# The last token block's final norm shared between VectorE, ScalarE and GpSimd, and the first products reordered, in a one-core encoder layer

## The chip, the cores and the metric

The kernel runs on one core of a Trainium2 chip. The time is the device time of one execution in microseconds; a version's time is the median of its runs. The engines are named as in the profile: PE (TensorE), ACT (ScalarE), DVE (VectorE), POOL (GpSimd), and SP (SyncE), whose queue issues most of the DMAs.

## What is computed

One encoder layer on 512 tokens of width 1024 in float32. Two token mixers (a windowed attention with sinks, and a mixture of dilated windows) are merged by sigmoid gates; a residual and a norm follow; then a SwiGLU feed-forward and the second residual and norm, whose output is the result:

```python
proj = h @ w_in[l]
qa, ka, va, qb, kb, vb = jnp.split(proj, SPLITS, axis=-1)
...
y = mixed @ w_out[l]
h = layer_norm(DN_ALPHA * h + y, ln1_g[l], ln1_b[l])
f = (jax.nn.silu(h @ w_ff_gate[l]) * (h @ w_ff_up[l])) @ w_ff_down[l]
h = layer_norm(DN_ALPHA * h + f, ln2_g[l], ln2_b[l])
```

with `layer_norm(x) = (x - mu) * rsqrt(var + eps) * g + b` over the 1024 columns.

## The kernel before

Every float32 operand is split into a high part (a rounded copy, on ACT or DVE) and a low part (the difference, on DVE), and a product is three matmuls: high by high, and each high by the other's low. A 128x512 tile is one `slot` (`sl` in the profile); weights come in units of 128x1024 from `wpack`, in halves of 512 columns.

The order of instructions on each engine is not written by hand. Every operation is handed to `Program.op` with the engines that may take it, a modelled cost, the tokens it reads and writes, and a priority; `Program.run` then plays the program through with these costs (a list scheduler), and each engine takes the ready operation with the lowest priority number. It also models the DMA path: `dma` holds two clocks, that of the issuing queue and that of the transfers, both 0 at the start. What the model thinks is ready first stands first in an engine's order, and on the chip each engine then keeps that order, whatever arrives first.

**The head.** The first three products, called k, q and r (the first unit of the keys, `U_KA`, and the first two of the queries, `U_QA` and `U_QA + 1`), run over the eight 128x512 tiles of x transposed (`xT`; `x` in the profile once they are split). Their weights' first halves come in pieces of 256 columns (`half_unit_by`, `CUTS`), with fixed priorities from the table `FIRST`; k's first piece is issued from ACT's queue, the rest from SP's. `FIRST["q", 0]` and `FIRST["r", 0]` begin with -999.7 and -999.6. The matmuls are those of L941. Before them PE runs eight matmuls on zeros (L409). After them come unit q2 (`feat_k`, L454 to L456), then the value weights (`token_values`, L610 to L629). The two rotary tables (`ropec`, `ropes`), the masks (`maska`, `maskb`) and the sinks (`nsink`) are loaded in the same stretch.

**The tail.** The last stage, `tok_major` with `fine` set, sums the down projection for four blocks `t` of 128 tokens, each with two column halves `j`, and norms each block when its sums are complete: residual (L1105), statistics (L1108, L1111), the root on ACT (L1113), `(z - mu) * g` on DVE (L1119, "centre" below), the reciprocal of the root on DVE (L1122), then `z * r + b` on DVE (L1134, "finish" below). In blocks 1 and 2 (`BY_POOL`) that finish is instead a scaling on ACT (L1127) and an addition of the bias on POOL (L1129). Each piece is stored by a DMA of SP's queue (`store`, L1493). For the last block the second half is cut in two pieces of 256 columns, so there are three pieces: 512, 256, 256.

At the program's end (L1595) each engine drains and all meet twice, with POOL as the one that collects and releases.

Of the kernel before, what the change touches and what calls it, by code (L numbers as in the profile page):

```python
# [12 lines left out]
AF = mybir.ActivationFunctionType  # L13
ALU = mybir.AluOpType

P = 128
S = 512
# [4 lines left out]
NR = 4  # L22
# [29 lines left out]
BRANCHES = "a0 a1 a2 b0 a3 b1 b2 a4 b3 b4 a5 b5 b6 a6 b7 a7"  # L52
N_BEGIN = 2
N_HALF = 3
N_LAST1, N_LAST, BY_POOL = 5, 4, (1, 2)
BANKS = dict(dense=3, s=2, tb=2, o=1, d=8)
UNITS = 2
D_BANK = "s"
SPIN = 4

CUTS = ((0, 256), (256, 512))
FIRST = {("k", 0): (-1000, -998.4), ("q", 0): (-999.7, -998.2), ("r", 0): (-999.6, -998.1),
         ("k", 1): (-997.7,), ("q", 1): (-997.5,), ("r", 1): (-997.4,),
# [34 lines left out]
class Program:  # L98
# [16 lines left out]
    def op(self, alts, fn, reads=(), writes=(), prio=0.0, after=(), abs_prio=None, moves=0.0):  # L115
        o = Op()
        o.urgent = self.urgent
        o.alts, o.fn = alts, fn
        o.prio = (self.T + prio if abs_prio is None else abs_prio, len(self.ops))
        o.ready, o.done, o.eng = 0.0, None, None  # L120
        deps = set(a for a in after if a is not None)
        for t in reads:
            deps.update(self.writer.get(t, ()))
        for t in writes:
            deps.update(self.writer.get(t, ()))
            deps.update(self.readers.get(t, ()))
        deps.discard(o)
        for t in reads:
            self.readers.setdefault(t, []).append(o)
        for t in writes:  # L130
            self.writer[t] = [o]
            self.readers[t] = []
        o.bufs, o.new = [], []
        o.strict, o.moves = self.strict, moves
        for t in list(reads) + list(writes):
            b = self.buf_of(t)
            if b not in o.bufs:
                o.bufs.append(b)
                b.users += 1
        o.succ = []  # L140
        o.left = len(deps)
        for d in deps:
            d.succ.append(o)
        self.ops.append(o)
        return o
# [25 lines left out]
    def run(self):  # L171
# [2 lines left out]
        pending = {e: [] for e in engines}  # L174
        times = [0.0]
        frees = []
        dma = [0.0, 0.0]

        def add(o):
            heapq.heappush(times, o.ready)  # L180
# [19 lines left out]
        while n_left:  # L200
# [5 lines left out]
            while frees and frees[0][0] <= now:  # L206
                _, _, b = heapq.heappop(frees)
# [68 lines left out]
def act(n, psum=False, extra=0):  # L276
    return (0.052 if psum else 0.094) + 0.000833 * n + 0.093 * extra


def dve(n, fast=False, extra=0.0):  # L280
    return 0.069 + (0.00074 if fast else 0.00104) * n + extra
# [7 lines left out]
def hybrid_layer(ctx: ExitStack, tc: tile.TileContext, wpack, xT, xtok, sink, bgate,  # L289
# [77 lines left out]
    def half_unit_by(u, j, cuts, prios):  # L367

        st, h, l = slot(F32, "ws"), slot(F32R, "whl"), slot(F32R, "whl")
        pieces[h] = pieces[l] = cuts  # L370
        for (c0, c1), ap in zip(cuts, prios):
            w = c1 - c0
            if ap == -1000:
                op([(ACT, 0.4)], lambda e, c0=c0, c1=c1: nc.scalar.dma_start(
                    st.t[:, c0:c1], wpack[u, :, j * S + c0:j * S + c1]), writes=[(st, c0)], abs_prio=ap,
                   moves=0.73 * w / S)
            else:
                op([(SP, 0.73 * w / S)], lambda e, c0=c0, c1=c1: nc.sync.dma_start(
                    st.t[:, c0:c1], wpack[u, :, j * S + c0:j * S + c1]), writes=[(st, c0)], abs_prio=ap)
            op(cp_alts(w), lambda e, c0=c0, c1=c1: copy(e, h.t[:, c0:c1], st.t[:, c0:c1]),  # L380
               reads=[(st, c0)], writes=[(h, c0), (l, "room", c0)], abs_prio=ap)
            op([(DVE, dve(w))], lambda e, c0=c0, c1=c1: nc.vector.tensor_tensor(
                l.t[:, c0:c1], st.t[:, c0:c1], f32(h.t[:, c0:c1]), op=ALU.subtract),
               reads=[(st, c0), (h, c0)], writes=[(l, c0)], abs_prio=ap)
        return h, l
# [672 lines left out]
    def ln_vectors(gsrc, bsrc, after):  # L1058
# [5 lines left out]
                res.append(b)  # L1064
        return res[0:2], res[2:4]

    def tok_major(nk, last, us_of, u0, g, b, finish, fine, alpha=ALPHA):

        acc = {(t, j): bank("d") for t in range(NR) for j in range(2)}

        def kmm(k, t, j, c0, c1, us, wu, ps):
            wh, wl = wu[j]

            def go(e):
                a0, a1 = us[0].t[:, t * P:(t + 1) * P], us[1].t[:, t * P:(t + 1) * P]
                o = ps.t[:, c0:c1]
                mm(o, a0, wh.t[:, c0:c1], start=(k == 0), stop=False, skip_group_check=True)  # L1077
                mm(o, a0, wl.t[:, c0:c1], start=False, stop=False, skip_group_check=True)  # L1078
                mm(o, a1, wh.t[:, c0:c1], start=False, stop=(k == nk - 1), skip_group_check=True)  # L1079

            op([(PE, 3 * pe(c1 - c0))], go, reads=[*us, wh, wl], writes=[ps])
            pr.T += 3 * pe(c1 - c0)

        for k in range(nk - last):
            us = us_of(k)
            wu = unit(u0 + k)
            for t in range(NR):
                for j in range(2):
                    kmm(k, t, j, 0, S, us, wu, acc[t, j])
        res = [(k, us_of(k), unit(u0 + k, LOOK if last < nk else LOOK_E)) for k in range(nk - last, nk)]  # L1090
        for t in range(NR):
            pr.urgent = t == NR - 1
            st = stats()
            pieces = [(0, 0, S), (1, 0, S)]
            if fine and t == NR - 1:
                pieces[1:] = [(1, 0, S // 2), (1, S // 2, S)]
            toks = []
            for n, (j, c0, c1) in enumerate(pieces):
                ps, z = bank("d") if c0 else acc[t, j], xt[t, j]
                for k, us, wu in res:  # L1100
                    kmm(k, t, j, c0, c1, us, wu, ps)
                tok = (z, c0)
                toks.append(tok)
                w = c1 - c0
                op([(DVE, dve(w))], lambda e, z=z, ps=ps, c0=c0, c1=c1: nc.vector.scalar_tensor_tensor(  # L1105
                    z.t[:, c0:c1], z.t[:, c0:c1], alpha, ps.t[:, c0:c1], op0=ALU.mult, op1=ALU.add),
                   reads=[z, ps], writes=[tok], prio=NOW)
                op([(DVE, dve(w))], lambda e, z=z, st=st, n=n, c0=c0, c1=c1: nc.vector.bn_stats(  # L1108
                    st.t[:, 6 * n:6 * n + 6], z.t[:, c0:c1]), reads=[tok], writes=[(st, n)], prio=NOW)
            np_ = len(pieces)  # L1110
            op([(DVE, 0.14)], lambda e, st=st, np_=np_: nc.vector.bn_aggr(st.t[:, 32:34], st.t[:, 0:6 * np_]),  # L1111
               reads=[(st, n) for n in range(np_)], writes=[(st, "a")], prio=NOW)
            op([(ACT, 0.2)], lambda e, st=st: nc.scalar.activation(  # L1113
                st.t[:, 34:35], st.t[:, 33:34], AF.Sqrt, bias=eps.t[:, 0:1]), reads=[(st, "a"), eps],
               writes=[(st, "s")], prio=NOW)
            for (j, c0, c1), tok in zip(pieces, toks):
                z = xt[t, j]
                op([(DVE, dve(c1 - c0, extra=0.06))], lambda e, z=z, st=st, j=j, c0=c0, c1=c1:
                   nc.vector.scalar_tensor_tensor(  # L1119
                       z.t[:, c0:c1], z.t[:, c0:c1], st.t[:, 32:33], g[j].t[:, c0:c1], op0=ALU.subtract,  # L1120
                       op1=ALU.mult), reads=[tok, (st, "a"), g[j]], writes=[tok], prio=NOW)
            op([(DVE, 0.1)], lambda e, st=st: nc.vector.reciprocal(st.t[:, 35:36], st.t[:, 34:35]),  # L1122
               reads=[(st, "s")], writes=[(st, "r")], prio=NOW)
            for (j, c0, c1), tok in zip(pieces, toks):
                z = xt[t, j]
                if fine and t in BY_POOL:
                    op([(ACT, act(S, extra=1))], lambda e, z=z, st=st: nc.scalar.activation(  # L1127
                        z.t, z.t, AF.Copy, scale=st.t[:, 35:36]), reads=[tok, (st, "r")], writes=[tok], prio=NOW)
                    op([(POOL, 1.25)], lambda e, z=z, j=j: nc.gpsimd.tensor_tensor(z.t, z.t, b[j].t, op=ALU.add),  # L1129
                       reads=[tok, b[j]], writes=[tok], prio=NOW)  # L1130
                    finish(t, j, c0, c1, tok)
                    continue
                op([(DVE, dve(c1 - c0, extra=0.06))], lambda e, z=z, st=st, j=j, c0=c0, c1=c1:
                   nc.vector.scalar_tensor_tensor(  # L1134
                       z.t[:, c0:c1], z.t[:, c0:c1], st.t[:, 35:36], b[j].t[:, c0:c1], op0=ALU.mult,
                       op1=ALU.add), reads=[tok, (st, "r"), b[j]], writes=[tok], prio=NOW)
                finish(t, j, c0, c1, tok)
        pr.urgent = False
# [461 lines left out]
```

## Time and profile before

| | us |
|---|---|
| median of 3 runs (lowest to highest) | 779.84 (779.28 to 780.75) |
| the profiled execution | 779.7 |
| its span, first to last instruction | 777.9 |
| busy in the span: PE, DVE, ACT, POOL | 766.2, 652.7, 479.7, 122.2 |

A row of the timeline gives start and length in us, the engine (with q: its sequencer, which only issues or waits), the line, the operation, tile written <- tiles read, the shapes, how many it merges, and in brackets the idle time ahead of it and what ended that. A row of busy times by stretch gives the stretch and its length, each engine's busy time and instructions, PE's granted clock, the DMA engines' mean share and GB/s. A row of groups gives line, engine, operation, tiles, shapes and count, then busy us and mean ns of one, then idle us before. A row of one line's sequencer instructions gives the count, min/median/max ns, and the first and last start.

### The profile page before, as it was taken

The numbers are of one execution on the slowest core, as the hardware profiler recorded it, in microseconds if no ns is written. First come the engines' busy times: TensorE is split into PE (matmuls) and PEld (weight loads), VectorE is DVE, ScalarE is ACT, GpSimd is POOL, SyncE is SP. The second block draws the span as 40 slices with busy tenths as digits, with TensorE's granted clock in tenths as the row PEclk, the third lists the DMA queues.
The fourth block names the chain that finished last, engine by engine and source line by source line (L and its number), as shares of the span: only waits on it lengthen the run. The fifth ranks groups of instructions, "written<-read, shape, count | busy, mean of one in ns | idle before, by whom it ended". The sixth has DMA issues, their size and how long they took to land.

```text
span 777.9 us, 13378 instructions
## 1 busy us (share of the span) xinstructions
PE 766.2 (99%) x4470; PEld 675.9 (87%) x4470; DVE 652.7 (84%) x1373; ACT 479.7 (62%) x1057; POOL 122.2 (16%) x288
## 2 busy tenths in 40 slices
PE   8999999999999999999999999999999999999995
PEld 6888888888888888888888899999999999999984
DVE  6378999888989898696686999797988889888697
ACT  6257785778787688693341767556655566555631
POOL 0011010101005204200020010232102331122002
PEclk9999999999999999999999999999999999999998
DMA  8745232203223224354472497699867987789102
GB/s 274 211 138 196 79 105 82 90 28 110 83 87 102 81 86 153 109 183 141 136 208 63 116 245 221 142 200 203 222 188 161 228 184 212 179 214 216 43 1 108
DMA packets 68848, 113.35 MB, mean 146 GB/s; under 512 B 8620, under 2 KB 17068, under 8 KB 68780
## 3 DMA queue, kind: packets, MB, share of 16 engines
q1 hardware_dynamic: 57116, 91.40, 36.4%
q0 software_dynamic: 11520, 20.98, 16.5%
q8 instruction: 35, 0.57, 0.3%
q14 instruction: 33, 0.27, 0.1%
q10 hardware_dynamic: 144, 0.13, 0.1%
HBM read 104.87 MB, written 4.72 MB: 141 GB/s over the span
## 4 chain that ended last, share of the span: by engine, by line
PE 96%; DVE 1%; ACT 1%; DMA 1%; issue 0%; SPq 0%; DVEq 0%; ACTq 0%
PE ps L454 10%; PE ps L455 10%; PE ps L456 10%; PE ps L1314 9%; PE ps L1313 9%; PE ps L1312 9%; PE ps L1441 4%; PE ps L1442 4%; PE ps L1443 4%; PE ps L675 3%; PE ps L1077 3%; PE ps L1079 3%; PE ps L1078 3%; PE ps L941 2%; PE ps L627 2%; PE ps L629 2%
## 5 line engine op out<-in xcount | busy, mean ns | idle before, releaser
L333 ACT ACTIVATE sl<-sl 128x512 fp32r<-128x512 f32 (+4 forms) x456 | 247.9, 571 | 79.7 <-DMA sl<-wpack 20.4
L1196 DVE TENSOR_TENSOR sl<-sl,sl 128x512 fp32r<-128x512 f32 (+3 forms) x304 | 169.8, 602 | 11.2 <-ACT sl L333 7.2
L333 ACT ACTIVATE sl<-ps 128x256 f32<-128x256 f32 (+4 forms) x188 | 81.6, 450 | 106.3 <-PE ps L1314 65.6
L454 PE MATMUL ps<-x,sl 128*128 128x512 f32 x280 | 110.9, 396 | 0.0
L455 PE MATMUL ps<-x,sl 128*128 128x512 f32 x280 | 109.5, 391 | 0.0
L456 PE MATMUL ps<-x,sl 128*128 128x512 f32 x280 | 109.3, 390 | 0.0
L354 DVE TENSOR_TENSOR sl<-sl,sl 128x512 fp32r<-128x512 f32 x114 | 75.5, 685 | 8.8 <-ACT sl L333 7.8
L1266 POOL DMA_DIRECT2D sl<-wpack x44 | 40.7, 1008 | 267.1 <-DMA sl<-wpack 144.1
L1312 PE MATMUL ps<-x,sl 128*128 128x256 f32 x264 | 74.8, 283 | 0.0
L1314 PE MATMUL ps<-x,sl 128*128 128x256 f32 x264 | 74.7, 283 | 0.0
L1313 PE MATMUL ps<-x,sl 128*128 128x256 f32 x264 | 74.7, 283 | 0.0
L1196 DVE TENSOR_TENSOR sl<-sl,ps 128x512 f32<-128x512 f32 (+1 forms) x78 | 47.3, 610 | 25.4 <-PE ps L1314 16.2
L456 PEld LDWEIGHTS ps<-x,sl 128*128 128x128 f32 x280 | 52.6, 188 | 11.5
L454 PEld LDWEIGHTS ps<-x,sl 128*128 128x128 f32 x280 | 52.7, 188 | 8.5
L455 PEld LDWEIGHTS ps<-x,sl 128*128 128x128 f32 x280 | 52.7, 188 | 8.3
L1313 PEld LDWEIGHTS ps<-x,sl 128*128 128x128 f32 x264 | 50.6, 192 | 0.5
L1312 PEld LDWEIGHTS ps<-x,sl 128*128 128x128 f32 x264 | 50.6, 192 | 0.5
L1314 PEld LDWEIGHTS ps<-x,sl 128*128 128x128 f32 x264 | 50.6, 192 | 0.0
L1314 PE MATMUL ps<-tw,sl 128*128 128x256 f32 x176 | 49.8, 283 | 0.0
L1313 PE MATMUL ps<-tw,sl 128*128 128x256 f32 x176 | 49.8, 283 | 0.0
L1314 PE MATMUL ps<-sl,sl 128*128 128x256 f32 x176 | 49.8, 283 | 0.0
L1313 PE MATMUL ps<-sl,sl 128*128 128x256 f32 x176 | 49.8, 283 | 0.0
(151 smaller groups left out, 1891.9 us busy)
## 6 DMA issues: line engine op xcount, KB each, us to landing
sl<-wpack SPq DMA_DIRECT2D x235, 256.0 KB, 3.7
sl<-wpack POOLq DMA_DIRECT2D x44, 256.0 KB, 5.6
wf<-wpack SPq DMA_DIRECT2D x36, 256.0 KB, 5.3
wf<-wpack POOLq DMA_DIRECT2D x36, 256.0 KB, 6.8
sl<-sl SPq DMA_DIRECT2D x88, 32.0 KB, 1.9
sl<-wpack SPq DMA_DIRECT2D x21, 128.0 KB, 4.3
sl<-xT SPq DMA_DIRECT2D x8, 256.0 KB
sl<-xtok SPq DMA_DIRECT2D x8, 256.0 KB, 2.9
```

Source lines behind the costliest of these rows:

```text
L333: nc.scalar.activation(dst, src, AF.Copy)
L354: op([(DVE, dve(S))], lambda e: nc.vector.tensor_tensor(l.t, src.t, f32(h.t), op=ALU.subtract), reads=[src, h], writes=[l], prio=prio, abs ...
L454: mm(o, a, x0, start=(k == 0), stop=False)
L455: mm(o, a, x1, start=False, stop=False)
L456: mm(o, b, x0, start=False, stop=(k == nk - 1))
L1196: op([(DVE, dve(w))], lambda e: nc.vector.tensor_tensor(dst(), x(), y(), op=o), reads=reads, writes=writes, prio=prio)
L1266: return op([(POOL, 1.0)], lambda e: nc.gpsimd.dma_start(dst.t, wpack[u, :, j * S:(j + 1) * S], accum_op=ALU.add), reads=[dst], writes=[ds ...
L1312: mm(o, wh, bh[k](), start=(first and k == 0), stop=False, skip_group_check=True)
L1313: mm(o, wh, bl[k](), start=False, stop=False, skip_group_check=True)
L1314: mm(o, wl, bh[k](), start=False, stop=(k == 3), skip_group_check=True)
L1441: mm(ps.t, x0, w[0].t, start=(first and m == 0), stop=False, skip_group_check=True)
L1442: mm(ps.t, x0, w[1].t, start=False, stop=False, skip_group_check=True)
```

## The change

In the last block's norm (`last_norm`, new) the first 384 columns (`CUT`) are centred first, scaled by ACT, given their bias by POOL and stored from ACT's queue. DVE takes the reciprocal right after that first centre, then centres and finishes the other half (512 columns) and the remaining 128 columns, which SP stores. The statistics are still taken in three pieces.

In the planner's model the transfers' clock starts at 2.2 us instead of 0, and the piece with priority -999.6 (r's first) costs 1.8 us more. These are numbers of the model alone; on the chip they change only the order in which instructions stand.

```diff
-N_LAST1, N_LAST, BY_POOL = 5, 4, (1, 2)
+N_LAST1, N_LAST, BY_POOL, CUT = 5, 4, (1, 2), 384
...
+SLOW = -999.6
...
-        dma = [0.0, 0.0]
+        dma = [0.0, 2.2]
...
-                op([(SP, 0.73 * w / S)], lambda e, c0=c0, c1=c1: nc.sync.dma_start(
+                op([(SP, 0.73 * w / S + 1.8 * (ap == SLOW))], lambda e, c0=c0, c1=c1: nc.sync.dma_start(
...
+    def last_norm(t, st, toks, g, b, finish):
+        z0, z1 = xt[t, 0], xt[t, 1]
+        lo_, mid, hi_ = (0, 0, CUT), (0, CUT, S), (1, 0, S)
+        need = {lo_: toks[:1], mid: toks[:1], hi_: toks[1:]}
+        def centre(part):
+            j, c0, c1 = part
+            z = xt[t, j]
+            op([(DVE, dve(c1 - c0, extra=0.06))], lambda e: nc.vector.scalar_tensor_tensor(
+                z.t[:, c0:c1], z.t[:, c0:c1], st.t[:, 32:33], g[j].t[:, c0:c1], op0=ALU.subtract, op1=ALU.mult),
+               reads=[*need[part], (st, "a"), g[j]], writes=[(z, "n", c0)], prio=NOW)
+        centre(lo_)
+        op([(DVE, 0.1)], lambda e: nc.vector.reciprocal(st.t[:, 35:36], st.t[:, 34:35]),
+           reads=[(st, "s")], writes=[(st, "r")], prio=NOW)
+        tok = (z0, "n", 0)
+        op([(ACT, act(CUT, extra=1))], lambda e: nc.scalar.activation(
+            z0.t[:, :CUT], z0.t[:, :CUT], AF.Copy, scale=st.t[:, 35:36]), reads=[tok, (st, "r")], writes=[tok],
+           prio=NOW)
+        op([(POOL, 1.25 * CUT / S)], lambda e: nc.gpsimd.tensor_tensor(
+            z0.t[:, :CUT], z0.t[:, :CUT], b[0].t[:, :CUT], op=ALU.add), reads=[tok, b[0]], writes=[tok], prio=NOW)
+        op([(ACT, 0.4)], lambda e: nc.scalar.dma_start(out[t, :, :CUT], z0.t[:, :CUT]), reads=[tok],
+           moves=0.73 * CUT / S)
+        centre(hi_)
+        centre(mid)
+        for j, c0, c1 in (hi_, mid):
+            z = xt[t, j]
+            tok = (z, "n", c0)
+            op([(DVE, dve(c1 - c0, extra=0.06))], lambda e, z=z, j=j, c0=c0, c1=c1: nc.vector.scalar_tensor_tensor(
+                z.t[:, c0:c1], z.t[:, c0:c1], st.t[:, 35:36], b[j].t[:, c0:c1], op0=ALU.mult, op1=ALU.add),
+               reads=[tok, (st, "r"), b[j]], writes=[tok], prio=NOW)
+            finish(t, j, c0, c1, tok)
...
+            if fine and t == NR - 1:
+                last_norm(t, st, toks, g, b, finish)
+                continue
```

Past the first rows (some 80 on an engine, 9 on PE) and up to the last block, every engine's rows are the same in both but for the numbers of lines and buffers. They differ in these places.

PE, first products. Before (`ps_115`, `ps_117`, `ps_123` are the sums of k, q, r; `x_94` and `x_111` the high and low parts of x; `sl_96`, `sl_102`, `sl_108` the high parts of the weights of k, q, r, and the next number of each the low part):

```order
L941 MATMUL ps_115<-x_94,sl_96 128x512
L941 MATMUL ps_117<-x_94,sl_102 128x512
L941 MATMUL ps_123<-x_94,sl_108 128x512
L941 MATMUL ps_115<-x_94,sl_97 128x512
L941 MATMUL ps_115<-x_111,sl_96 128x512
L941 MATMUL ps_117<-x_94,sl_103 128x512
L941 MATMUL ps_123<-x_94,sl_109 128x512
L941 MATMUL ps_117<-x_111,sl_102 128x512
L941 MATMUL ps_123<-x_111,sl_108 128x512
```

Now (`ps_115` is q, `ps_119` k, `ps_138` r; the line is L942):

```order
L942 MATMUL ps_115<-x_101,sl_105 128x512
L942 MATMUL ps_119<-x_101,sl_108 128x512
L942 MATMUL ps_119<-x_101,sl_109 128x512
L942 MATMUL ps_119<-x_113,sl_108 128x512
L942 MATMUL ps_115<-x_101,sl_106 128x512
L942 MATMUL ps_115<-x_113,sl_105 128x512
L942 MATMUL ps_138<-x_101,sl_132 128x512
L942 MATMUL ps_138<-x_101,sl_133 128x512
L942 MATMUL ps_138<-x_113,sl_132 128x512
```

r's first product was the third and is the seventh; the four products of k and q with a low part stand ahead of it. On the other engines k's first high part is now made by DVE, as its second cast, instead of by ACT as its first.

SP, the loads behind the last tile of x. Before (the first two `wpack` rows are the halves of q2; L610 are value weights, each `x2` one pair):

```order
L341 DMA bg<-bgate 128x16
L341 DMA sl_165<-wpack 128x512
L341 DMA sl_169<-wpack 128x512
L610 DMA sl_176<-wpack 128x2x128 x2
L610 DMA sl_188<-wpack 128x2x128 x2
L341 DMA sl_199<-ropec 128x1x512
L610 DMA sl_205<-wpack 128x2x128 x2
L610 DMA sl_214<-wpack 128x2x128 x2
L341 DMA sl_223<-maska 128x384
L341 DMA sl_231<-ropes 128x1x512
L341 DMA nsink<-sink 128x16
L341 DMA ident<-identd 128x128
```

Now:

```order
L342 DMA bg<-bgate 128x16
L342 DMA sl_141<-ropec 128x1x512
L342 DMA sl_145<-maska 128x384
L342 DMA sl_150<-ropes 128x1x512
L342 DMA nsink<-sink 128x16
L342 DMA sl_163<-wpack 128x512
L342 DMA ident<-identd 128x128
L342 DMA sl_174<-wpack 128x512
L611 DMA sl_182<-wpack 128x2x128 x2
L342 DMA sl_192<-maskb 128x512
L611 DMA sl_201<-wpack 128x2x128 x2
L611 DMA sl_215<-wpack 128x2x128 x2
```

Both rotary tables, the first mask and the sinks moved ahead of q2's halves and of all value weights. On DVE the sinks' scaling and the copies of two finished sums (k and r, before k and q) stand among the first low parts of the value weights, where they stood behind the third of them; ACT copies the other sum, four rows earlier than before.

DVE, the last block, from its statistics to the end. Before (`sl_4536` and `sl_4548` are the block's two halves, `st_9391` its statistics):

```order
L1111 BN_AGGR st_9391<-st_9391 128x2
L1119 SCALAR_TENSOR_TENSOR sl_4536<-sl_4536,st_9391,sl_8557 128x512
L1119 SCALAR_TENSOR_TENSOR sl_4548<-sl_4548,st_9391,sl_8560 128x256 x2
L1122 RECIPROCAL st_9391<-st_9391 128x1
L1134 SCALAR_TENSOR_TENSOR sl_4536<-sl_4536,st_9391,sl_8569 128x512
L1134 SCALAR_TENSOR_TENSOR sl_4548<-sl_4548,st_9391,sl_8584 128x256 x2
```

Now (L1078 are the centres, L1098 the finishes):

```order
L1147 BN_AGGR st_9391<-st_9391 128x2
L1078 SCALAR_TENSOR_TENSOR sl_4536<-sl_4536,st_9391,sl_8557 128x384
L1083 RECIPROCAL st_9391<-st_9391 128x1
L1078 SCALAR_TENSOR_TENSOR sl_4548<-sl_4548,st_9391,sl_8560 128x512
L1078 SCALAR_TENSOR_TENSOR sl_4536<-sl_4536,st_9391,sl_8557 128x128
L1098 SCALAR_TENSOR_TENSOR sl_4548<-sl_4548,st_9391,sl_8584 128x512
L1098 SCALAR_TENSOR_TENSOR sl_4536<-sl_4536,st_9391,sl_8569 128x128
```

The reciprocal moved ahead of two centres, and 384 columns of the finish are gone. Those stand now at the end of ACT's rows (a scaling of 128x384 and, behind it, the DMA that stores them and waits for POOL) and of POOL's (one addition of 128x384, which waits for ACT, as its last work). SP's last rows were three stores of this block (512, 256, 256 columns) and are two (512, 128).

## The prediction

> I read the page's busy shares and chain first, then the busy times by stretch, then both ends of the timeline, since the diff touches only these.
>
> ```profile
> PE 766.2 (99%) x4470; PEld 675.9 (87%) x4470; DVE 652.7 (84%) x1373; ACT 479.7 (62%) x1057; POOL 122.2 (16%) x288
> PE 96%; DVE 1%; ACT 1%; DMA 1%; issue 0%; SPq 0%; DVEq 0%; ACTq 0%
> 0.00:4.80 4.80, 3.59 (x8) 1.04 (x8) 0.71 (x4) 1.74 (x3) 0.20 (x4) 1.00 0.53 165
> 4.80:7.00 2.20, 0.95 (x3) 0.55 (x3) 1.41 (x4) 0.68 (x2) 0.00 (x0) 1.00 0.75 229
> 22.90:769.70 746.80, 745.76 (x4392) 661.18 (x4390) 634.79 (x1338) 465.95 (x1033) 121.02 (x284) 1.00 0.53 142
> 769.70:777.90 8.20, 0.03 (x1) 0.00 (x0) 4.24 (x10) 0.29 (x1) 1.01 (x1) 0.72 0.35 128
> ```
>
> **What bounds it.** PE. From 22.9 to 769.7 it is busy for 745.76 of 746.80 us, so the middle is one unbroken string of products, which starts earlier if the first products end earlier. Time off that string lies at the two ends: 1.25 us idle between 4.8 and 7.0, and 8.2 us after the last product. The span is 777.9, the profiled execution 779.7, so 1.8 lies around the span; the median of the runs, 779.84, is 0.14 above this execution. I sum against 779.7 and add the 0.14 at the end.
>
> **The head.** The timeline of the first products (PE, and the casts that feed it on ACT and DVE):
>
> ```profile
> 4.35 0.72 ACT L333 ACTIVATE sl<-sl 128x256 fp32r<-128x256 f32 x2 [1.89 <-DMA sl<-wpack]
> 4.82 0.92 PE L941 MATMUL ps<-x,sl 128*128 128x512 f32 x2
> 5.14 0.68 DVE L430 TENSOR_TENSOR x<-sl,x 128x512 fp32r<-128x512 f32 x1
> 5.74 0.42 DVE L382 TENSOR_TENSOR sl<-sl,sl 128x256 fp32r<-128x256 f32 x1
> 6.49 0.42 ACT L333 ACTIVATE sl<-sl 128x256 fp32r<-128x256 f32 x1 [1.43 <-DMA sl<-wpack]
> 6.94 0.42 DVE L382 TENSOR_TENSOR sl<-sl,sl 128x256 fp32r<-128x256 f32 x1 [0.79 <-ACT sl L333]
> 6.96 16.17 PE L941 MATMUL ps<-x,sl 128*128 128x512 f32 x70 [1.23 <-ACT sl L333]
> 7.17 0.63 ACT L333 ACTIVATE x<-sl 128x512 fp32r<-128x512 f32 x1 [0.26 <-DMA sl<-xT]
> 22.97 0.39 PE L454 MATMUL ps<-x,sl 128*128 128x512 f32 x1
> ```
>
> PE runs two products, k's and q's, and then stands before r's, whose weights have landed when ACT casts them at 6.49. Four products of k and q with the low parts already have their operands (DVE is done with x's low part at 5.82 and with q's at 6.16), but stand behind r in PE's order. The change puts them ahead: six products before r, 66 instead of 70 after it. One takes (22.97 - 6.96)/70 = 0.229, so four are 0.92. Something is late next: r's three end at about 7.65, and the second x tile is cast only at 7.17 + 0.63 = 7.80, so about 0.1 goes back on that wait after the hop. I take a gain of 0.82. Its bounds are 0.92 (no new wait) and 0 (the wait moves whole to a later load, the last rival). k's first cast moves from ACT to DVE: ACT's second cast here becomes its first, and DVE's new one stands ahead of x's low part; even 0.5 later these six end before 6.9, because the 1.25 idle covers them.
>
> The same planner numbers move loads in SP's queue: both halves of q2's weights and the value weights now stand behind both rotary tables, the mask and the sinks.
>
> ```profile
> 12.94 1.99 ACT L333 ACTIVATE x<-sl 128x512 fp32r<-128x512 f32 x3
> 14.29 0.80 SPq L341 DMA_DIRECT2D sl<-ropec  x1
> 15.05 1.41 ACT L333 ACTIVATE sl<-sl 128x512 fp32r<-128x512 f32 x2
> 20.88 0.63 ACT L333 ACTIVATE sl<-sl 128x512 fp32r<-128x512 f32 x1 [2.25 <-DMA sl<-wpack]
> 25.28 0.63 ACT L333 ACTIVATE sl<-sl 128x512 fp32r<-128x512 f32 x1 [2.56 <-DMA sl<-wpack]
> ```
>
> Loads of 256 KB come 0.66 apart (1.99 for three casts). A rotary table costs the loads behind it 2.25 and 2.56. q2's first half was cast at 15.05; behind both tables and 192 KB of mask (three quarters of 0.66) that becomes 15.05 + 2.25 + 2.56 + 0.5 = 20.4, and done at 21.0. PE now wants it at 22.97 - 0.82 = 22.15, so 1.1 of cover is left, and I cost the move at nothing. With the cover gone it costs one for one. The value weights follow at the same 0.66 for a pair of 128 KB, and are wanted after 24 more products, 5.5 later, one pair for three products (0.69). The bias and sink copies and the two evacuations that change places on DVE and ACT wait for nobody that PE needs in this stretch. From there to the last block the engines' rows are the same, so I carry the 0.82 to the end.
>
> **The tail.** Times as in the trace of before; all shift with the head.
>
> ```profile
> 765.87 1.42 DVE L1119 SCALAR_TENSOR_TENSOR sl<-sl,st,sl 128x512 f32<-128x512 f32 x2
> 767.39 1.34 ACT L1127 ACTIVATE sl<-sl,st 128x512 f32<-128x512 f32 x2 [1.23 <-DVE st L1122]
> 768.19 1.29 POOL L1129 TENSOR_TENSOR sl<-sl,sl 128x512 f32<-128x512 f32 x1 [2.21 <-ACT sl L1127]
> 768.19 2.51 POOL L1129 TENSOR_TENSOR sl<-sl,sl 128x512 f32<-128x512 f32 x2 [2.21 <-ACT sl L1127]
> 770.68 0.24 DVE L1111 BATCH_NORM_AGGREGATE st<-st 128x2 f32<-128x18 f32 x1
> 770.95 1.54 DVE L1119 SCALAR_TENSOR_TENSOR sl<-sl,st,sl 128x512 f32<-128x512 f32 x3
> 772.41 0.16 DVE L1122 RECIPROCAL st<-st 128x1 f32<-128x1 f32 x1
> 772.61 1.54 DVE L1134 SCALAR_TENSOR_TENSOR sl<-sl,st,sl 128x512 f32<-128x512 f32 x3
> 773.39 1.29 SPq L1493 DMA_DIRECT2D out<-sl  x3
> L1119 DVE SCALAR_TENSOR_TENSOR sl<-sl,st,sl 128x512 f32<-128x512 f32 x5 | 3.6, 750 | 0.1
> L1119 DVE SCALAR_TENSOR_TENSOR sl<-sl,st,sl 128x256 f32<-128x256 f32 x2 | 0.9, 480 | 0.0
> GB/s 0 0 0 0 0 0 0 0 0 0 0 0 225 451 389 369 328 389 410 267 348 369 359 318 348 328 297 52 0 0 0 0 0 0 0 0 0 0 0 0
> L1493 SPq DMA_DIRECT2D out<-sl x9: 332/333/390, 758.2 to 774.3; - x9
> SPq L1595 <- DMA out<-sl: 1.5, 1, 1.5
> L1595 POOLq DRAIN  x1: 6397/6397/6397, 768.8 to 768.8; - x1
> L1595 POOLq EVENT_SEMAPHORE  x4: 17/17/17, 776.9 to 777.8; - x4
> ```
>
> By 750 ns for 512 columns and 480 for 256, 384 columns take 0.615 and 128 take 0.345, each next one starting about 0.08 before the end. DVE: 384 columns centred from 770.95, the reciprocal from 771.48 to 771.64 (before 772.41), 512 centred to 772.31, 128 to 772.57, then the 512 finished by 773.25 and the 128 by 773.51 (before: the last at 774.15). In SP's queue three issues from 773.39, the last at 774.3, become two, at 773.28 and 773.7. ACT scales from 771.67 for 0.61 (two of 512 take 1.34, one about 0.72); POOL, 0.08 behind as at 768.19, adds from 772.36. Its 512 took 1.29, so 384 is between 0.96 (by columns) and 1.29: I take 0.98, to 773.34. ACT then issues its store at 773.4; nothing but ACT's end stands behind that wait.
>
> DVE is thus done 0.64 sooner, but the stores are not. The row of GB/s (slices of 0.1 from 773.0) shows 0.52 MB that flow without a pause from 774.2 to 775.75, about 340 GB/s: the bytes set the end. The same bytes follow a first issue that is 0.11 earlier, so I take 0.1 gained; bounds are 0 and 0.6 (the last issue). SP's 1.5 us wait for them ends as much sooner.
>
> The other half of the end is POOL. It drains before all engines meet; the drain, issued at 768.8, ends at 775.2, which is 4.5 after the end of its last add (768.19 + 2.51 = 770.70), and POOL passes the meeting at 776.9, when SP comes: 1.7 of cover. If the drain keeps its 4.5 behind a last add that ends at 773.34, it ends at 777.84, 0.94 after the old meeting. The 1.0 after it is unchanged. So the tail is 0.94 longer, and the stores' 0.1 no longer counts. Bounds: -0.1 (POOL's drain not bound to its work) and +1.8 (6.4 from its issue at 772.3). I take +0.94, because the nearest row measures an end behind the same kind of add.
>
> Sum: -0.82 + 0.94 = +0.1; 779.7 + 0.1 + 0.14 = 779.9. The two halves cancel.
>
> **Rivals.**
> A, the drain does not follow POOL. For it: DVE's finals with two SBUF inputs run until 774.15, and the drain ends 1.0 later; it may have waited for those or for something else that is fixed. Against: behind POOL's last add nothing else of POOL's is left that could take the time. Then only -0.82 - 0.1 counts: 778.9. The Trainium skill, page VectorE: DVE Perf Modes, section The DRAIN you can't avoid, puts such drains at about 12 ns on all engines, which would give this rival's time. By that rule, the trace does not agree: this one took 6397 ns.
>
> B, slower: POOL's add and DVE's last two steps cannot run together, and POOL goes last. It would start at 773.51, end at 774.5, its drain at 779.0: +2.1 - 0.82 = +1.3, 781.1. It is slower at all once POOL's add ends after 773.22 on this scale, and by over 0.2% after 774.8. If POOL goes first instead, from 772.57 to 773.55, it is +0.3, 780.2. For: they overlap fully only after the change. Against: at 765.87 DVE began such a step 0.1 before POOL's add of that time ended, and its pair took 1.42, not stretched; the overlap is too short to tell. The Trainium skill, page SBUF — State Buffer, section SBUF: two separate sides, says that a VectorE instruction with two SBUF inputs and a GpSimd one that reads SBUF lock each other out for a whole instruction. By that rule the price is this rival's; no run here shows it yet.
>
> C, the loads: the tables cost over 1.1 more than the two waits show, and PE stands before q2. Then the head gives nothing or loses: 780.8 at a gain of 0, over 781.4 if PE waits another 0.6.
>
> **Chances.** Forecast 0.43, with its own range of 779.6 to 780.4; A 0.35; B with POOL last 0.14; C 0.08. A measurement of this kernel tells about 0.2%, 1.56 us, from no change: under 778.3 or over 781.4. Nearly all cases lie between. Faster: only A with a run or two off, 0.06. Slower: half of C and a late B, 0.09. Same: 0.85. The range takes in A and B: 778.6 to 781.3.
>
> **What would show it.** Right: six products before r's; the first of q2 near 22.15 without idle before it; the last statistics on DVE end near 770.1; POOL's last add of 128x384 about 1.0 long; POOL's drain ends some 4.5 after it and after SP's last wait; the span within 0.3 of 777.9. Wrong: a drain that ends soon after the add, with SP last (A); POOL's add over 1.3, or a DVE final of over 1 us or begun late (B); PE idle before q2 or between 22 and 28 (C).

## The result, and the profile after

The changed kernel takes 782.39 us (median of 7 runs, 781.71 to 782.77) against 779.84 for the kernel before (7 runs beside it, 779.09 to 780.75): a ratio of 1.0029, 95% interval 1.002 to 1.0039 (ratios here go by all executions; the two medians alone give 1.0033). The forecast was 779.9, no change; the kernel became 2.55 us slower. The profiled execution took 782.45 with a span of 780.6, which is 2.7 more than the span before. Its busy shares, from the page:

```profile
PE 766.9 (98%) x4470; PEld 676.0 (87%) x4470; DVE 653.1 (84%) x1373; ACT 480.3 (62%) x1057; POOL 123.1 (16%) x289
```

Shares tell next to nothing here. The busy times by stretch, cut where the changed kernel waits, tell more:

```profile
4.80:7.00 2.20, 2.01 (x6) 1.60 (x7) 1.56 (x4) 0.64 (x3) 0.00 (x0) 1.00 0.91 305
...
22.00:49.20 27.20, 27.20 (x121) 22.33 (x119) 15.37 (x27) 11.23 (x19) 0.84 (x3) 1.00 0.52 149
49.20:52.50 3.30, 1.20 (x4) 0.59 (x4) 3.15 (x5) 3.25 (x7) 1.80 (x4) 1.00 0.27 79
52.50:771.40 718.90, 717.87 (x4268) 638.11 (x4266) 618.81 (x1311) 454.22 (x1013) 118.23 (x278) 1.00 0.53 142
771.40:780.60 9.20, 0.01 (x1) 0.00 (x0) 4.35 (x9) 0.91 (x2) 2.02 (x2) 0.65 0.31 114
```

The idle time between 4.8 and 7.0 is gone (1.25 before, 0.19 now). A new one stands between 49.2 and 52.5: PE is busy for 1.20 of 3.30 us. And the stretch behind the last product is 9.2 long, where it was 8.2. Three terms make the 2.7: about -0.95 at the head, +2.6 from 49 us to the end of PE's string, +1.04 in the tail.

**The head's wait is gone, as was said.** From the timeline after:

```profile
4.52 0.78 ACT L334 ACTIVATE sl<-sl 128x256 fp32r<-128x256 f32 x2 [2.05 <-DMA sl<-wpack]
4.99 17.16 PE L942 MATMUL ps<-x,sl 128*128 128x512 f32 x72 [0.20 <-ACT sl L334]
20.13 0.63 ACT L334 ACTIVATE sl<-sl 128x512 fp32r<-128x512 f32 x1 [4.95 <-DMA sl<-wpack]
21.99 0.39 PE L455 MATMUL ps<-x,sl 128*128 128x512 f32 x1
```

All 72 products of k, q and r run as one string, and q2 begins at 21.99 instead of 22.97. q2's first cast, 20.13 to 20.76, is 1.2 ahead of PE. So the place that the prediction named for a loss through the moved loads did not lose anything.

The 0.98 is not the new order's alone. r's weights also landed earlier in this execution: the second of ACT's two casts, from 4.88, is r's, and before it began at 6.49. That moment differs from execution to execution, with the same order of those first loads (5.26 in the run with the products alone, 6.46 in the run with the small operation, both below). With PE's old order and r cast from 4.9, in the run with the loads alone, q2 began at 22.34; in the ten profiles with the new order it began between 21.92 and 22.60. So one pair of profiles cannot size the gain; the medians at the end of the experiments do it better.

**The loss stands at the first gate unit**, the unit behind the value products (L455 to L457, before L454 to L456). The waits of PE after, from 45 to 56 us, with the total, the count and the longest; before there was none in this stretch:

```profile
PE ps L455 <- ACT sl L334: 1.6, 1, 1.6
PE ps L457 <- DVE sl L355: 0.5, 1, 0.5
```

PE waits for the gate's first cast and then for its first low part. What makes them late shows when the timeline is followed back. Before:

```profile
32.80 1.14 SPq L483 DMA_DIRECT2D sl<-sl  x2
36.98 0.73 DVE L494 STREAM_SHUFFLE sl<-sl 128x512 f32<-128x512 f32 x1
41.81 1.28 ACT L333 ACTIVATE sl<-sl 64x512 fp32r<-64x512 f32 x2 [7.17 <-DMA sl<-sl]
43.75 3.91 ACT L333 ACTIVATE sl<-sl 64x512 fp32r<-64x512 f32 x6
48.31 3.24 ACT L333 ACTIVATE sl<-sl 128x512 fp32r<-128x512 f32 x6
49.44 3.70 DVE L354 TENSOR_TENSOR sl<-sl,sl 128x512 fp32r<-128x512 f32 x6
50.17 0.39 PE L454 MATMUL ps<-x,sl 128*128 128x512 f32 x1
50.62 0.39 PE L456 MATMUL ps<-x,sl 128*128 128x512 f32 x1
```

After:

```profile
34.76 1.15 SPq L484 DMA_DIRECT2D sl<-sl  x2
38.95 0.73 DVE L495 STREAM_SHUFFLE sl<-sl 128x512 f32<-128x512 f32 x1
43.78 1.29 ACT L334 ACTIVATE sl<-sl 64x512 fp32r<-64x512 f32 x2 [10.11 <-DMA sl<-sl]
45.71 3.91 ACT L334 ACTIVATE sl<-sl 64x512 fp32r<-64x512 f32 x6
50.27 3.24 ACT L334 ACTIVATE sl<-sl 128x512 fp32r<-128x512 f32 x6
50.95 0.50 PE L455 MATMUL ps<-x,sl 128*128 128x512 f32 x1 [1.60 <-ACT sl L334]
51.41 3.13 DVE L355 TENSOR_TENSOR sl<-sl,sl 128x512 fp32r<-128x512 f32 x5
52.18 0.50 PE L457 MATMUL ps<-x,sl 128*128 128x512 f32 x1 [0.50 <-DVE sl L355]
```

Read from the top: SP issues small copies (16x512) of the finished sums for the rotary step; DVE shuffles and rotates them; SP copies them back; ACT casts the eight rotated pieces (64x512); and only behind these does ACT cast the gate's weights (128x512), though they were loaded right behind the value weights (in a run below their cast is done at 33.4). Each row of SP, DVE and ACT is 1.96 or 1.97 later than its row before. (The profile puts the shuffle's wait down to a load of weights; by the kernel the shuffle reads only what the copies wrote, and it starts 2.9 to 3.2 after the last of them in these two kernels, in the first three runs below and with flat tables.) The first row is late because the copies stand in the same queue as the loads. SP's waits for the tables and the mask between 9 and 36 us, before:

```profile
SPq L341 <- DMA sl<-ropec: 1.4, 1, 1.4
```

and after:

```profile
SPq L611 <- DMA sl<-ropes: 2.0, 1, 2.0
...
SPq L611 <- DMA sl<-ropec: 1.1, 1, 1.1
SPq L342 <- DMA sl<-maska: 0.5, 1, 0.5
```

SP keeps eight transfers under way; the ninth issue waits for the one eight places back (the second value weight stands eight places behind the first table and waits for it, the next two issues wait for the mask and for the second table). With both tables and the mask ahead of the value weights, the gaps between SP's issues from 9.2 us to the last rotary copy sum to 5.6 instead of 3.7, less the 0.04 that stands between any two, and after 19.64 SP issues one command after another until 38.6 (0.37 to 0.84 each, and one of 1.76), so nothing is caught up.

**The tail.** Instructions of the last block, from the timeline and by form, after:

```profile
774.05 1.03 POOL L1089 TENSOR_TENSOR sl<-sl,sl 128x384 f32<-128x384 f32 x1 [1.67 <-ACT sl L1086]
774.16 1.74 DVE L1098 SCALAR_TENSOR_TENSOR sl<-sl,st,sl 128x512 f32<-128x512 f32 x2
```

```profile
L1098 DVE SCALAR_TENSOR_TENSOR sl<-sl,st,sl 128x512 f32<-128x512 f32 x1 | 1.5, 1479 | 0.0
...
L1089 POOL TENSOR_TENSOR sl<-sl,sl 128x384 f32<-128x384 f32 x1 | 1.0, 1032 | 1.7 <-ACT sl L1086 1.7
L1078 DVE SCALAR_TENSOR_TENSOR sl<-sl,st,sl 128x512 f32<-128x512 f32 x1 | 0.7, 731 | 0.0
```

POOL's sequencer and SP's at the program's end (count, min/median/max ns, first and last start):

```profile
L1634 POOLq EVENT_SEMAPHORE  x4: 17/17/17, 779.6 to 780.5; - x4
L1634 POOLq DRAIN  x3: 40/102/5528, 774.0 to 780.1; - x3
...
L1634 SPq DRAIN  x3: 7/7/13, 778.5 to 779.8; - x3
```

POOL's drain begins at 774.02 and ends 5.53 later, at 779.55: 4.46 after its addition, which runs from 774.05 to 775.09. Before it was the same 4.46 (770.70 to 775.2). SP is ready at 778.5, and everything waits another 1.0 for POOL. (DVE's drain ends at 775.95, only 0.05 after DVE's last step.) And DVE's finish of 512 columns, which begins 0.10 after POOL's addition, takes 1479 ns where a step of that size takes 731.

### The profile page after: what moved, and what is told of

The parts are those of the page before. It is cut to its first block, busy times and chain, and to the rows that moved or that the text cites. A ratio compares the mean times of both kernels' runs of the same rounds, so it can differ in the third digit from the quotient of the medians.

```text
span 780.6 us, 13365 instructions
## 1 busy us (share of the span) xinstructions
PE 766.9 (98%) x4470; PEld 676.0 (87%) x4470; DVE 653.1 (84%) x1373; ACT 480.3 (62%) x1057; POOL 123.1 (16%) x289
## 4 chain that ended last, share of the span: by engine, by line
PE 96%; ACT 2%; DVE 1%; DMA 0%; issue 0%; SPq 0%; DVEq 0%; ACTq 0%
PE ps L457 10%; PE ps L455 10%; PE ps L456 10%; PE ps L1353 9%; PE ps L1352 9%; PE ps L1351 9%; PE ps L1480 4%; PE ps L1481 4%; PE ps L1482 4%; PE ps L676 3%; PE ps L1115 3%; PE ps L1113 3%; PE ps L1114 3%; PE ps L942 2%; PE ps L628 2%; PE ps L629 2%
## 5 line engine op out<-in xcount | busy, mean ns | idle before, releaser
L334 ACT ACTIVATE sl<-sl 128x512 fp32r<-128x512 f32 (+3 forms) x455 | 247.4, 572 | 82.4 <-DMA sl<-wpack 20.7
L455 PE MATMUL ps<-x,sl 128*128 128x512 f32 x280 | 111.0, 397 | 1.6 <-ACT sl L334 1.6
L457 PE MATMUL ps<-x,sl 128*128 128x512 f32 x280 | 109.4, 391 | 0.5 <-DVE sl L355 0.5
L456 PE MATMUL ps<-x,sl 128*128 128x512 f32 x280 | 109.5, 391 | 0.0
L1235 DVE TENSOR_TENSOR sl<-sl,ps 128x512 f32<-128x512 f32 (+1 forms) x78 | 47.4, 611 | 25.4 <-PE ps L1353 16.3
L457 PEld LDWEIGHTS ps<-x,sl 128*128 128x128 f32 x280 | 52.6, 188 | 12.4 <-DVE sl L355 0.9
L455 PEld LDWEIGHTS ps<-x,sl 128*128 128x128 f32 x280 | 52.7, 188 | 10.4 <-ACT sl L334 2.0
L456 PEld LDWEIGHTS ps<-x,sl 128*128 128x128 f32 x280 | 52.8, 188 | 8.3
```

The source lines that it names most:

```text
L334: nc.scalar.activation(dst, src, AF.Copy)
L455: mm(o, a, x0, start=(k == 0), stop=False)
L456: mm(o, a, x1, start=False, stop=False)
L457: mm(o, b, x0, start=False, stop=(k == nk - 1))
L1235: op([(DVE, dve(w))], lambda e: nc.vector.tensor_tensor(dst(), x(), y(), op=o), reads=reads, writes=writes, prio=prio)
```

## The experiments

Theory L: the moved loads hold SP, the rotary copies behind them come late, and with them all that stands behind the rotated pieces on ACT and DVE. Theory D: the end waits for a drain of POOL that ends 4.46 after its last work. Each run was timed beside the kernel before, whose median was then 779.69 to 779.95. The ratios are to it.

**The first products alone.**

```diff
+        todo = sorted(todo, key=lambda o: o[1][0] == "r") if k == 0 else todo
...
+                after=done[:6] if k == 0 and w == "r" else ()))
```

> Kernel before with only the order of the first nine products changed (six of k and q, then r's three); every load, cast and the tail stay where they were. Theory L (the moved loads made the rotary copies in SP's queue, the rotary casts on ACT and behind them the gate's first cast 1.96 later): PE reaches the gate unit 0.95 earlier, at 49.22, where its first cast is done at 48.94 and its first low part at 50.13, as before; PE waits only for that low part (wanted at 49.67): 0.5. So 779.84 - 0.95 + 0.5 = 779.4. Rival E (the stall comes from PE being early, the loads' order costs nothing): the same stall as in the changed kernel, 2.5, so 779.84 - 0.95 + 2.5 = 781.4.

779.68 (779.19 to 780.41), ratio 0.9999 (0.999 to 1.0007). PE is 0.87 ahead when it reaches the gate unit, and 0.13 ahead two products later, with this wait between 45 and 56 us:

```profile
PE ps L456 <- DVE sl L354: 0.5, 1, 0.5
```

So it is the low part alone, as theory L said, and not the 2.5 of the rival. Of the 0.74 lost, some 0.4 is the low part of before (done at 50.13, wanted 0.87 sooner than 50.62); the rest is that this run's rotary copies ended 0.4 later than in the kernel before. The head's gain is lost even where no load is moved, because the kernel before has only 0.49 to spare there: the low part is done at 50.13 (49.44 + 0.69) and used at 50.62.

**The moved loads alone**: the two planner numbers, with PE's order of before.

```diff
+        todo = [todo[i] for i in (0, 1, 2, 3, 6, 4, 5, 7, 8)] if k == 0 else todo
...
+                after=done[-1:] if k == 0 else ()))
```

> The two planner numbers as in the changed kernel, but the first nine products held in the order of before, and the tail of before. Theory L: PE is at its old place (the gate unit at 50.17) and the gate's first cast and low part come 1.96 late; PE's third product there starts at about 52.2 instead of 50.62, so 1.56 later: 781.4. Rival E: PE is not early, so no stall: 779.8.

782.25 (780.98 to 784.4), ratio 1.0035 (1.0022 to 1.0048). With PE in its old order there is the same kind of stall: PE waits 1.4 and 0.5 at the gate, is 1.63 late at the gate's third product and 1.75 soon after. PE came some 0.6 early here too, because r's weights landed early, but coming early cannot make it late in the end. The rival is out: the loads cost by themselves. The median is 2.4 above that of the kernel before, and not 1.56: four executions lie between 780.98 and 781.57, as expected, and four between 782.93 and 784.4. The profile is of the first four; what the others spend more on is not shown.

**Both planner numbers, tail of before.**

```diff
-        dma = [0.0, 0.0]
+        dma = [0.0, 2.2]
...
+                op([(SP, 0.73 * w / S + 1.8 * (ap == SLOW))], lambda e, c0=c0, c1=c1: nc.sync.dma_start(
```

> Both planner numbers with the tail of before. Theory L: the gate unit's low part sets the time whatever PE does ahead of it, so the same as with the loads alone: +1.56 to 1.7, 781.4 to 781.5, with a stall of 2.5 at the gate unit and PE's first products 0.95 earlier. Rival E gives the same here; the pair before tells them apart.

781.43 (780.27 to 783.63), ratio 1.0027 (1.0017 to 1.0036), 1.6 above the kernel before, as expected. The stall itself was 0.9 and not 2.5: PE came only 0.5 ahead, and the copies ended 0.8 sooner than in the changed kernel. Set side by side, the profiles show one rule. PE's third product at the gate starts a fixed time after SP's last rotary copy, wherever PE was:

| | last rotary copy ends | third gate product | apart |
|---|---|---|---|
| products alone | 34.35 | 50.49 | 16.1 |
| loads alone | 35.90 | 52.25 | 16.4 |
| planner numbers | 35.09 | 51.49 | 16.4 |
| changed kernel | 35.90 | 52.18 | 16.3 |

**The new tail alone**, planner numbers of before.

> Only the new last norm, the planner's numbers as before. Theory D (POOL's drain ends 4.46 after the end of POOL's last addition, and the meeting waits for it): +1.04, 780.9, POOL passing the meeting about 1 us later than SP comes. Rival S (the cost of the tail is the stretched finish on DVE, 1.48 instead of 0.75, and so the late stores): SP's last wait would end with POOL's or after it. If neither, 779.8.

780.83 (780.31 to 782.3), ratio 1.0015 (1.0006 to 1.0024). The profiled execution is the longest of its eleven (its first products took 1.4 longer), so only its tail is read, within itself: the drain ends at 779.31, 4.46 after POOL's addition, and SP was ready at 778.3. The DVE finish is stretched here too (1.48), but the end is POOL's: theory D. The two halves, +1.6 and +1.0, add up to the 2.55 of the whole.

**The gate's first half in slots of its own**, so that its cast stands ahead of the rotary casts.

```diff
+        cls = None if u == U_GATE and j == 0 else "whl"
+        st, h, l = slot(F32, "ws"), slot(F32R, cls), slot(F32R, cls)
```

> The changed kernel, with the first half of the first gate unit's weights split into two slots of the general class instead of the weights' own; its cast on ACT and its low part on DVE then stand ahead of the rotary casts instead of behind them, and nothing else moves but one load of SP that comes earlier. Theory L: the rotary copies stay 1.9 late, but PE no longer waits for them; the 2.5 at the gate unit goes: 782.4 - 2.5 = 779.9, which is before - 0.95 for the head + 1.04 for the tail. Rival N (the rotated pieces themselves come too late, at the next unit or at the first scores): the 2.5 comes back within the next 90 us of PE, 782.4.

781.76 (780.93 to 782.99), ratio 1.0028 (1.0019 to 1.0037): a miss. The gate's wait is gone, but a wait of the same kind was put 17 us ahead of it:

```profile
32.05 1.15 ACT L334 ACTIVATE sl<-sl 128x512 fp32r<-128x512 f32 x2 [3.21 <-DMA sl<-wpack]
33.25 0.49 PE L629 MATMUL ps<-sl,x 128*128 128x512 f32 x1 [0.67 <-ACT sl L334]
34.05 0.50 PE L630 MATMUL ps<-sl,x 128*128 128x512 f32 x1 [0.31 <-DVE sl L617]
```

The gate's cast now stood one place ahead of the last value weight's, and held it until its own load had landed. Putting it one place later:

```diff
+        split(st, h, l, prio=-look, hold=[(l, "room")], after=va_ops if own else ())
```

> As the run with the gate's first half in slots of its own, but its cast stands behind the cast of the last value weight on ACT (there it stood ahead of it, waited 3.2 us for its own load, and PE stood 1.6 before the eighth value product instead of 2.5 before the gate). Theory L: neither of the two stalls is left: 782.4 - 2.5 = 779.9. Rival N (the rotated pieces come too late for a later unit): 781.5 or more, with the stall behind the gate unit.

781.01 (780.06 to 782.26), ratio 1.0012 (1.0003 to 1.0021). PE passes the gate 1.0 ahead of the kernel before, without a wait. Of the 2.5, 1.4 came back; 0.3 of the lead is lost near 53 us and 0.8 at the first attention block, around 72 us. The rotary copies of this run ended at 36.29, 2.4 later than before. That is half a miss, as the rival had it:

```profile
72.08 0.50 PE L746 MATMUL ps<-sl,sl 128*128 128x512 f32 x1 [0.36 <-DVE sl L685]
```

What holds the step on DVE there was not followed further.

**Flat tables**: the changed kernel, with the rotary tables laid out in 128 rows and loaded plainly.

```diff
-        load(t_, src[0:16].unsqueeze(0).broadcast_to([8, 16, S]), abs_prio=ap)
+        load(t_, src, abs_prio=ap)
```

> The changed kernel, with both rotary tables laid out in full (128 rows each) and loaded with a plain 128x512 load, instead of 16 rows that the load repeats eight times. Order and bytes written are the same. Theory B (the repeated rows are what lands slowly, and SP's queue with its eight loads under way waits for them): both tables land in about 0.7 each as the other 256 KB loads do, SP's waits fall from 5.6 to about 2 to 3.7, the last rotary copy comes 2 or more earlier, and the stall falls from 2.5 to 0.5: 780.4. Rival Q (eight places are filled with small loads, whatever the form of the tables): the last rotary copy stays at 35.9 and the time at 782.4.

780.2 (779.65 to 780.47), ratio 1.0004 (0.9995 to 1.0013): 2.2 faster than the changed kernel, without one instruction moved. So it is the tables' loads that cost, and not the few copies that the planner numbers also moved on DVE and ACT. What the DMA engines moved from 13 to 14.5 us, while the tables land, first after, then with flat tables:

```profile
DMA packets 230, 0.31 MB, mean 206 GB/s; under 512 B 66, under 2 KB 126, under 8 KB 230
```

```profile
DMA packets 465, 0.59 MB, mean 390 GB/s; under 512 B 163, under 2 KB 242, under 8 KB 465
```

The repeated tables bring the rate down to about half of what flat ones leave in this stretch, where the two differ most; from 10 to 20 us it is 270 against 328. SP's waits for the tables are gone from its list, the last rotary copy ends at 32.54 instead of 35.90:

```profile
31.39 1.15 SPq L484 DMA_DIRECT2D sl<-sl  x2
```

And PE waits for nothing between 9 and 75 us. Theory B holds. The Trainium skill, page DMA: Bandwidth & Descriptors, section Rules for kernel authors, says that a leading broadcast of c copies, fewer than 16, confines a DMA to c engines; here c is 8, and a rate of about half from 13 to 14.5 us agrees with it. The trace does not tell the engines apart, and flat tables are also read from eight times as many addresses, so which of the two it is stays open.

**The changed kernel without POOL's addition** (the bias of 384 columns is left out).

```diff
-        op([(POOL, 1.25 * CUT / S)], lambda e: nc.gpsimd.tensor_tensor(
-            z0.t[:, :CUT], z0.t[:, :CUT], b[0].t[:, :CUT], op=ALU.add), reads=[tok, b[0]], writes=[tok], prio=NOW)
```

> The changed kernel without POOL's addition in the last block (the bias of those 384 columns is left out); ACT stores right behind its scaling. Theory D + lock: the drain goes back to POOL's addition of block 2 and ends before SP comes, DVE's 512-column finish takes 0.75 instead of 1.48, so the last store is issued 0.6 to 0.7 earlier: 782.4 - 1.04 - 0.5 = 780.8 to 780.9. Without the lock (the finish stays 1.48): 781.35. If the drain does not follow POOL: 782.4.

780.79 (779.75 to 782.44), ratio 1.0012 (1.0003 to 1.0021), with the planner's loss still in it. The finish:

```profile
L1096 DVE SCALAR_TENSOR_TENSOR sl<-sl,st,sl 128x512 f32<-128x512 f32 x1 | 0.7, 747 | 0.0
```

747 instead of 1479, and the drain ends at 776.33, before SP is ready (777.2).

**One small operation of POOL behind the kernel before's last finish.**

```diff
+            if fine and t == NR - 1:
+                op([(POOL, 0.1)], lambda e, z=z, st=st: nc.gpsimd.tensor_copy(st.t[:, 40:41], z.t[:, S - 1:S]),
+                   reads=[tok], writes=[(st, "x")], prio=NOW)
```

> The kernel before with one more operation: after the last finish on DVE, POOL copies one column (128x1) into a spare column of the statistics. Theory D (the drain ends 4.46 after POOL's last work, whatever that is): POOL's copy at 774.2 to 774.3, the drain until 778.75 instead of 775.2, the meeting 1.9 later: 781.7. Rival W (the drain's length goes with the amount of work behind which it stands, so a small one is short): the drain ends before SP comes at 776.8: 779.8.

781.95 (781.79 to 782.15), ratio 1.0024 (1.0014 to 1.0034). From the timeline and the sequencer's list:

```profile
774.42 0.18 POOL L1139 COPY st<-sl 128x1 f32<-128x1 f32 x1 [3.50 <-DVE sl L1134]
```

```profile
L1598 POOLq DRAIN  x3: 93/187/4667, 774.4 to 779.9; - x3
```

The drain runs from 774.40 to 779.06, 4.46 after a copy of one column ended at 774.60. A copy of one column is followed by the same 4.46 as an addition of a whole tile, so rival W is out. The copy costs 2.3 us of the kernel.

**Keeping the head's gain.** Three versions of the kernel before with the products reordered and its own tail: with the gate's own slots (cast behind the value weights'), with flat tables, and with both.

> Kernel before, with the first nine products reordered, the gate's first half in slots of its own and its cast behind the last value weight's; loads and tail as before. Theory L: the 0.87 to 0.95 that the head gives and that was lost again at the gate's first low part is kept: 778.9. Rival N: lost again at a later wait, 779.7.

> Kernel before, with the first nine products reordered and the rotary tables laid out in full and loaded plainly; the gate's casts as before. Theory L with B: the rotary copies end 1 to 2 earlier than 33.94, so the gate's first low part is done by 49.1 and is wanted at 49.67: the head's gain is kept, 778.9. Rival Q: the gate's low part at 50.4 as with the products alone, 779.7.

> Both of the two runs before in one, tail as before. Theory L: both take away the same wait, so together no more than either: 778.9. If the loads still cost PE something elsewhere in the head: 778.5.

779.17 (0.9989, 0.9981 to 0.9998), 778.92 (0.9989, 0.998 to 0.9997) and 778.95 (0.9987, 0.9979 to 0.9996). None shows a wait of PE between 9 and 75 us, and PE's last product starts 0.4 to 0.7 earlier than before. Both remedies take away the same wait, and together they give no more than one. All three beat both kernels: the one before by 0.8 to 1.0, the changed one by over 3. No run has either remedy with PE's old order, so that the gain is the new order's alone is argued, from the kernel before having no wait of PE between 9 and 75 us that a remedy could take away.

## Why the prediction was wrong, and where it was right

- **The head, -0.82**: right in kind, and in size by the 0.8 to 1.0 that the last three runs keep. That q2 began 0.98 earlier in the profile is partly luck: the sum took the landing of r's weights as fixed (cast from 6.49), and in that execution they were cast from 4.88.
- **The step that failed: "I cost the move at nothing".** It followed the moved loads to q2 and to the value weights, where the cover of 1.1 was right (1.2 measured). It did not follow what else uses SP's queue. The rotary copies stand behind the same loads, and the gate's cast stands behind the rotated pieces on ACT. The term measured +2.5 at the gate (with both planner numbers +1.6 in the median, and the 0.9 that the head had given).
- **The second half of that failure: "the engines' rows are the same, so I carry the 0.82 to the end".** Equal order is not equal time. The profile of before held the row that speaks against it: a low part done at 50.13 and used at 50.62. A gain of 0.82 ahead of a spare of 0.49 cannot be carried past it; the run with the products alone gave 0.13 behind that place.
- **POOL's drain, +0.94**: right, +1.04, by the mechanism named. Rival A is out: six profiles show 4.46 behind an addition of 512 columns, of 384, and a copy of one. The Trainium skill, page VectorE: DVE Perf Modes, section The DRAIN you can't avoid, gives some 12 ns for the drains that stand ahead of and behind a kernel (preamble and postamble), on all engines. For POOL's drain at the kernel's last line this does not hold; SP's drains there took 7 to 13 ns.
- **"The bytes set the end"**: wrong, hidden behind the drain. SP's wait ends 2.0 after the last store's issue before (774.29 to 776.28), 1.9 after it in the changed kernel (776.09 to 777.97) and without POOL's addition (774.82 to 776.69), for 128 KB, 64 KB and 64 KB: the last issue sets it.
- **Rival B**: its lock was there, with POOL first. DVE's finish was stretched, by 0.73, so the last store was issued 0.7 later than DVE's own work needed. It cost nothing only because the drain ended later still. By the rule of the Trainium skill, page SBUF — State Buffer, section SBUF: two separate sides, whichever starts first keeps the port for a whole instruction. The trace agrees in who waits (1479 against 747 ns, and the finish ends 0.55 after POOL's addition). It does not agree in full: a wait until the addition's end and then all of the 747 would make 1.68, and 1.48 was measured.
- **Rival C**: the right culprit, the tables, at the wrong place. Its condition, a cost of more than 1.1 before q2, was not met; the loss came 27 us later, in another engine's order.
- **"Loads of 256 KB come 0.66 apart"**: the three casts stand back to back on ACT, so that row shows ACT's pace and not the loads'. The DMA engines moved 380 GB/s from 12 to 14 us, which makes 0.69, so the sum did not suffer.

## What to carry to other kernels

When loads change places in a queue, follow everything that the queue issues after them, the small copies between two steps of the computation above all, up to the place where the engine that sets the time meets their results. A gain at the head is worth no more than the smallest spare on the way: look in the trace of before for an operand that is done just ahead of its use. And at a kernel's end count GpSimd's drain from the end of its last work.

## What the runs showed of the hardware

- GpSimd's last drain ended 4.46 us after its last work in every profile read for it, for an addition of 128x512 as for a copy of 128x1. Work that is given to it last costs this much unless something else takes longer.
- Tables loaded by repeating 16 rows eight times held the transfers at 206 GB/s in a stretch where flat ones of the same size let them run at 390.
- A VectorE step with two SBUF inputs took 1479 ns beside a GpSimd addition and 731 to 747 without it, while the GpSimd addition took 1032 ns for 384 columns (1264 for 512 in the block before). No run has that addition alone, so whether it was stretched too is not shown.
